# A planned order for the attention stage of a two-layer HGRN2 and dilated-attention block

## The chip, the core and the metric

The kernel runs on one core of a Trainium2 chip. Its time is the device time of one execution in microseconds. The engines named below are TensorE (PE, matrix products; its weight loads are PEld), VectorE (DVE), ScalarE (ACT), GpSimd (POOL) and SyncE (SP), whose queue issues most of the transfers from HBM.

## The reference, cut to what matters

One sequence of 512 tokens with 1024 channels goes through two layers. Each layer is a mixer and a gated feed-forward network (FFN), and each of the two is wrapped in a conditioned norm and a gate: six vectors per layer (shift, scale and gate for the mixer, the same for the FFN) come from the conditioning input and `ada_w`. They are written (layer, number) below, (1,4) for instance. Layer 0's mixer is HGRN2; layer 1's is attention in three groups:

```python
DILATED_GROUPS = ((128, 1), (512, 4), (2048, 16))      # window, dilation
def dilated_attention_mixer(u, cos, sin, w_in, w_out):
    proj = (u @ w_in).reshape(B, S, N_GROUPS, 3, ATT_HEADS, ATT_HEAD_DIM)
    for gi, (window, dilation) in enumerate(DILATED_GROUPS):
        q = apply_partial_rope(proj[:, :, gi, 0], cos, sin) * scale
        k = apply_partial_rope(proj[:, :, gi, 1], cos, sin)
        o_g, lse_g = dilated_group_attention(q, k, proj[:, :, gi, 2], window, dilation)
    wts = softmax(stack(lses), axis=0)                 # shares of the three groups
    o = einsum('gbsh,gbshd->bshd', wts, stack(outs))
    return o.reshape(B, S, D_MODEL) @ w_out

def swiglu_ffn(u, w_in, w_out):
    gate, up = split(u @ w_in, 2)
    return (silu(gate) * up) @ w_out
```

There are 8 heads of 128 channels. The rotary turn touches the first 32 of them. The FFN's inner width is 2816.

## The kernel before, in words

**Weights.** Each fp32 operand is split in a high half of type fp32r (a cast on ACT) and a low half (a subtraction on DVE), and each product is three products: high by high, high by low, low by high (`three`). The weights pass through a `Stream`: an item list in a fixed order, two raw buffers of 1 MB (`raw`), filled by SP, and three places of split weights (`hi`, `lo`). An item of kind `w` is a weight; `ada` is 1 MB of `ada_w`, which DVE reduces in four chunks into an accumulator (L257, L259); `do` and `rows` finish a conditioning vector. `weave(ws, others, first, every)` puts one of the others behind every so many weights. `take(ahead)` works through the items up to the weight wanted plus `ahead` more, by default two, and returns the split weight. So a plain `take()` also issues the splits of the next two weights.

**First FFN.** Its second product takes eleven weights, 48 products of 512 columns each. Between the first nine stand eight `ada` items, for (1,1) and (1,0).

**Attention stage.** Values of group 0 are made first. Values of groups 1 and 2 are made in two halves by a seven-product scheme (`seven_values`, L1395). Then, head by head and group by group, a block of 48 products makes query and key (24 each; `block` into a bank `mm`). `qk_evac` copies the rotary rows apart into `shared` (L1704) and the rest to `qk` (L1705), both on ACT. `turn_pair` turns the rows on DVE (L1712 to L1715), and ACT copies them back into `qk` (L1720 for group 0, L1722 for the other two). `scores` makes the scores (PE L1743, L1761 into a bank `a`), DVE takes the maxima (L1748, L1763), ACT the exponentials (L1753, L1772). `weights_of` computes the groups' shares (`wM`, `wE`, `wZ`, with an exponential on ACT, L1785), `merge_r` and `merge_n` scale by them on DVE (L1798, L1805), `flip` transposes on PE (L1810) and evacuates on ACT (L1815) or DVE (L1817), `pv_r` and `pv_n` sum over values (L1836, L1837, L1846, L1848) into `oT`. Each of these steps is put off by a fixed number of half blocks (`fl.add(n + 3, ...)`). The tile scheduler, which simulates a timeline while it emits (`schedule_with_timeline_sim`), sets the order of instructions on each engine here. The `ada` items of (1,2), (1,4) and (1,3) are woven in among the heads' weights.

**The seam.** `mixer_out` multiplies `oT` by `attn_w_out`, four weights. It makes the first five column blocks while head 7's last steps, given to it as `tail`, still run. Its order is fixed by hand. `cut(kt)` splits one column block of `oT` into `oh` (ACT, L434) and a low half (DVE, L435); `three` in this stage is L438 to L440:

```python
for kt in range(3):
    cut(kt)
for kt in range(KT):
    if kt % 4 == 0:
        w = st.take(0)
    ...
    for t in range(NT):
        prods(y0[t], t, kt, w)
```

and the loop over heads ahead of it takes its weights with `whi, wlo = st.take()`.

Of the kernel before, what the change touches and what calls it, by code (L numbers as in the profile page):

```python
# [1 line left out]

# [35 lines left out]
class Stream:  # L38
# [73 lines left out]
    def whole(self):  # L112

        assert self.items[self.done][0] in WHOLE
        self.fill()
        self.done += 1
        return self.raw.pop(self.done - 1)
# [10 lines left out]
    def take(self, ahead=None):  # L128
        ahead = self.parts - 1 if ahead is None else ahead
        k = min(self.taken + ahead, len(self.wpos) - 1)  # L130
        stop = next((i for i in range(self.done, len(self.items)) if self.items[i][0] in WHOLE), len(self.items))
        self.process_to(min(self.wpos[k] + 1, stop))
        if k == len(self.wpos) - 1:
            self.process_to(stop)
        self.taken += 1
        return self.ready.pop(0)

# [21 lines left out]
def block_kernel(tc, x, c, positions, ada_w, ada_b, norm_g, hgrn_w_in, lower, hgrn_norm_g, hgrn_w_out,  # L159
# [8 lines left out]
    with ExitStack() as ctx:  # L168
# [95 lines left out]
        def ada_item(l, v, hf, kq):  # L264
            src = ada_w[l, kq * 512:(kq + 1) * 512, v * D + hf * 512:v * D + (hf + 1) * 512]
            return ("ada", src.rearrange("(k p) n -> p k n", p=P), ada_chunk(l, v, hf, kq))
# [43 lines left out]
        def fin_item(l, v, hf):  # L310
            if v not in (2, 5):
                return ("do", None, col_fin(l, v, hf))
# [3 lines left out]
            return ("rows", (b, n), row_fin(l, v, hf))  # L316
# [62 lines left out]
        items += weave(f0b[:9], ada_seq((1, 1), (1, 0)), 0, 0.9) + f0b[9:]  # L379
# [4 lines left out]

        def aqk(g, hd):
            return ("w", tuple(AW[:, (g * 3 + k) * D + hd * P:(g * 3 + k) * D + (hd + 1) * P].rearrange(
                "(k p) n -> p k n", p=P) for k in range(2)))
# [14 lines left out]
        def woven(others, every):  # L402
            items.extend(weave(at, others, 0, every))
            at.clear()
# [6 lines left out]
        late = ada_seq((1, 2), (1, 4), (1, 3))  # L411
# [3 lines left out]
        woven(late[:8], 1.5)  # L415
# [4 lines left out]
        woven(late[8:], 1.3)  # L420
# [16 lines left out]
        def three(ps, ah, al, bh, bl, start, stop):  # L437
            pe.matmul(ps, ah, bh, start=start, stop=False)  # L438
            pe.matmul(ps, ah, bl, start=False, stop=False)  # L439
            pe.matmul(ps, al, bh, start=False, stop=stop)  # L440
# [942 lines left out]
        def seven_values(dsts, apart, th, tl):  # L1383


            C = lambda raw, c: V4(raw)[:, :, c * 256:c * 256 + 256]
            G = lambda t, o: V4(t[:, o * 1024:(o + 1) * 1024])
            u_of = lambda r, c: lambda kt, n: [a[:, r * 4 + kt, c * 256 + n * P:c * 256 + (n + 1) * P] for a in apart]
            t_of = lambda i: lambda kt, n: [a[:, i, kt, n * P:(n + 1) * P] for a in (th, tl)]
            raws, tiles = {}, {}  # L1390

            def cut(i, tile, o, k, c):
                hi, lo = tiles[i, tile]
                src = C(raws[i][k], c)
                act.copy(G(hi, o), src)  # L1395
                dve.tensor_sub(G(lo, o), src, G(hi, o).bitcast(F32))

            def place(i, tile):
                tiles[i, tile] = st.part_tiles(V0)

            def prepare(i, step):
                if i >= len(dsts):
                    return
                if step == 0:
                    raws[i] = [st.whole(), st.whole()]
                    place(i, 0)
                    cut(i, 0, 0, 0, 0)
                    cut(i, 0, 1, 1, 1)
                elif step == 1:
                    place(i, 1)  # L1410
                    cut(i, 1, 0, 1, 0)
                    a, b = raws[i]
                    dve.tensor_add(C(b, 1), C(b, 1), C(a, 1))
                    dve.tensor_add(C(a, 1), C(a, 1), C(a, 0))
                    dve.tensor_add(C(a, 0), C(a, 0), C(b, 1))
                    dve.tensor_add(C(b, 0), C(b, 0), C(a, 0))
                    cut(i, 1, 1, 0, 0)
                elif step == 2:
                    place(i, 2)
                    cut(i, 2, 1, 0, 1)  # L1420
                    st.fill(1)
                    cut(i, 2, 0, 1, 1)
                else:
                    place(i, 3)
                    cut(i, 3, 0, 1, 0)
                    raws.pop(i)
                    st.fill()

            def run(ps, i, tile, o, us):
                hi, lo = tiles[i, tile]  # L1430
                for n in range(2):
                    for kt in range(4):
                        w = slice(o * 1024 + kt * 256, o * 1024 + (kt + 1) * 256)
                        three(ps[:, n * 256:(n + 1) * 256], *us(kt, n), hi[:, w], lo[:, w], kt == 0, kt == 3)

            H2 = lambda a: a.rearrange("p (n c) -> p n c", n=2)
            for step in range(3):
                prepare(0, step)
            for i, dst in enumerate(dsts):
                X, Y, Z, U = (dst[:, t:t + 2, c:c + 256] for c in (0, 256) for t in (0, 2))  # L1440
                m1 = bank("mm")
                run(m1, i, 0, 0, u_of(0, 0))
                act.copy(X, H2(m1))
                m4 = bank("a")
                run(m4, i, 0, 1, t_of(2))
                prepare(i, 3)
                m2 = bank("mm")
                run(m2, i, 1, 0, u_of(1, 0))
                m6 = bank("mm")
                run(m6, i, 1, 1, t_of(3))  # L1450
                dve.tensor_add(Y, X, H2(m6))
                dve.tensor_add(X, X, H2(m2))
                prepare(i + 1, 0)
                m5 = bank("mm")
                run(m5, i, 2, 0, t_of(0))
                m7 = bank("mm")
                run(m7, i, 2, 1, t_of(1))
                dve.scalar_tensor_tensor(Z, Y, -1.0, H2(m7), op0=OP.mult, op1=OP.subtract)
                dve.tensor_add(Y, Y, H2(m5))
                dve.tensor_sub(U, Z, H2(m5))  # L1460
                dve.tensor_sub(Z, Z, H2(m4))
                prepare(i + 1, 1)
                m3 = bank("mm")
                run(m3, i, 3, 0, u_of(1, 1))
                dve.tensor_add(Y, Y, H2(m3))
                prepare(i + 1, 2)

# [383 lines left out]
        fl.n = 0  # L1851
        for kind, g, i in order:
            if kind == "v":
                if g == 1:

                    for fn in fl.at.pop(fl.n, []):
                        fn()
                    seven_values(V[1:], apart, th, tl)
                    if i:
                        act.dma_start(V[0], v_away)  # L1860
                continue
            if g == 0:
                heads[i] = {}
                n = fl.n
                fl.add(n + 3, lambda i=i: scores(i, 0))
                fl.add(n + 5, lambda i=i: scores(i, 1))
                fl.add(n + 7, lambda i=i: scores(i, 2))
                fl.add(n + 9, lambda i=i: (merge_r(i), merge_n(i)))
                fl.add(n + 10, lambda i=i: flips_r(i))
                fl.add(n + 11, lambda i=i: pv_r(i))  # L1870
                fl.add(n + 11, lambda i=i: flips_n(i))
                fl.add(n + 12, lambda i=i: pv_n(i))
# [8 lines left out]
        fl.at.clear()  # L1881
# [37 lines left out]
```

## Time and profile before

| | |
|---|---|
| runs | 1510.45, 1510.66 (median), 1511.49 us |
| profiled execution | 1511.44 us, of which the span takes 1509.4 |
| mean granted TensorE clock | 0.997 |
| first FFN's second product | about 537 to 649 us of the span |
| group 0's values | about 690 to 727 us |
| other values and heads | 727 to 1107 us |
| output product with head 7's end | from 1107 us |

Rows of a stretch read: from and to, length, then busy time (and instructions) of PE, PEld, DVE, ACT and POOL, the mean granted TensorE clock as a share of full speed, the share of time that the DMA engines were busy, GB/s. Timeline rows read: start, length, engine, line, operation and tiles, count, and in brackets the idle time ahead of it with what ended it. Rows of waits: what waited, for whom, us in total, times, the longest. Rows of groups: line, engine, operation, forms, count, busy us and mean ns, idle time before.

### The profile page before, as it was taken

To read this page: it belongs to the slowest core of one execution; us is meant where nothing else is said; L and a number is where in the kernel's file an instruction comes from. 1 tells how busy PE (TensorE), PEld (TensorE's weight loads), DVE (VectorE), ACT (ScalarE), POOL (GpSimd) and SP (SyncE) were. 2 spreads that over 40 slices of the span, in tenths; PEclk is the share of its full clock that TensorE was granted. 3 is DMA by queue.
4 is the path that set the end of the run, shared out by engine and by line. 5 is a ranking of instruction groups with operands and counts; after the bars stand their busy time and mean duration, and the time that the engine had idled before them with its cause. 6 is when DMAs were issued, how large, how long until landed. Compare 5 with 4: busy or idle time off the path is not lost. (4 is left out here: it accounts for less than half of the span.)

```text
span 1509.4 us, 23492 instructions
## 1 busy us (share of the span) xinstructions
PE 1493.7 (99%) x9231; PEld 1309.7 (87%) x9231; DVE 1040.2 (69%) x1807; ACT 746.6 (49%) x1321; POOL 199.0 (13%) x174
## 2 busy tenths in 40 slices
PE   8999999999999999999999999999999999999998
PEld 6777888898999988888988888988888899999886
DVE  4587768486888876577668766686466978887533
ACT  4443433362555542376546666356655555555231
POOL 1011211030111101040001110011002211110100
PEclk9999999999999999999999999999999999999999
DMA  9553444125333356424166540365213333334531
GB/s 309 166 183 126 156 152 168 56 85 167 101 109 107 107 200 213 155 108 141 57 183 191 151 120 29 123 185 141 84 52 117 100 97 112 112 112 141 199 108 56
DMA packets 206942, 199.14 MB, mean 132 GB/s; under 512 B 6840, under 2 KB 164720, under 8 KB 206576
## 3 DMA queue, kind: packets, MB, share of 16 engines
q1 hardware_dynamic: 203856, 190.87, 40.3%
q10 hardware_dynamic: 1952, 6.65, 1.2%
q8 instruction: 72, 1.18, 0.3%
q0 software_dynamic: 1024, 0.13, 0.2%
q14 instruction: 38, 0.31, 0.1%
HBM read 192.31 MB, written 5.31 MB: 131 GB/s over the span
## 5 line engine op out<-in xcount | busy, mean ns | idle before, releaser
L88 ACT CAST hi<-raw 128x2048 fp32r<-128x2048 f32 x68 | 129.7, 1907 | 199.1 <-DMA raw<-in_ffn_w_out_dram 60.8
L89 DVE TENSOR_TENSOR lo<-raw,hi 128x2048 fp32r<-128x2048 f32 x68 | 161.5, 2377 | 96.2 <-ACT hi L88 96.2
L438 PE MATMUL ps_mm<-apart,hi 128*128 128x512 f32 x384 | 151.4, 394 | 0.0
L439 PE MATMUL ps_mm<-apart,hi 128*128 128x512 f32 x384 | 151.2, 394 | 0.0
L440 PE MATMUL ps_mm<-apart,lo 128*128 128x512 f32 x384 | 150.6, 393 | 0.0
L438 PE MATMUL ps_mm<-uh,hi 128*128 128x512 f32 (+1 forms) x400 | 146.3, 366 | 0.0
L439 PE MATMUL ps_mm<-ul,hi 128*128 128x512 f32 (+1 forms) x400 | 144.3, 361 | 1.0 <-DVE ul L538 1.0
L440 PE MATMUL ps_mm<-uh,lo 128*128 128x512 f32 (+1 forms) x400 | 144.6, 361 | 0.0
L438 PE MATMUL ps_mm<-hi,oh 128*128 128x512 f32 x240 | 94.0, 392 | 0.0
L853 PE MATMUL ps_mm<-th,hiq 128*128 128x256 f32 x340 | 93.9, 276 | 0.0
L853 PE MATMUL ps_mm<-tl,hiq 128*128 128x256 f32 x340 | 93.9, 276 | 0.0
L853 PE MATMUL ps_mm<-th,loq 128*128 128x256 f32 x340 | 93.9, 276 | 0.0
L439 PE MATMUL ps_mm<-lo,oh 128*128 128x512 f32 x240 | 93.4, 389 | 0.0
L438 PEld LDWEIGHTS ps_mm<-uh,hi 128*128 128x128 f32 x400 | 75.5, 189 | 19.7 <-issue 8.4
L844 DVE TENSOR_TENSOR loq<-raw,hiq 128x1024 fp32r<-128x1024 f32 x68 | 80.2, 1221 | 16.8 <-ACT hiq L840 16.8
L439 PEld LDWEIGHTS ps_mm<-ul,hi 128*128 128x128 f32 x400 | 75.6, 189 | 12.1 <-DVE ul L538 1.4
L440 PEld LDWEIGHTS ps_mm<-uh,lo 128*128 128x128 f32 x400 | 75.5, 189 | 11.4
L824 POOL TENSOR_TENSOR raw<-raw 128x512 f32<-128x512 f32 x34 | 45.1, 1328 | 305.1 <-DVE spare L820 131.3
L440 PEld LDWEIGHTS ps_mm<-apart,lo 128*128 128x128 f32 x384 | 72.2, 188 | 14.5
L439 PEld LDWEIGHTS ps_mm<-apart,hi 128*128 128x128 f32 x384 | 72.2, 188 | 14.2
L438 PEld LDWEIGHTS ps_mm<-apart,hi 128*128 128x128 f32 x384 | 72.2, 188 | 14.1
L259 DVE SCALAR_TENSOR_TENSOR shared<-raw,cond,shared 128x512 f32<-128x512 f32 x98 | 73.2, 747 | 12.9 <-DMA raw<-in_ada_w_dram 11.9
(440 smaller groups left out, 4183.5 us busy)
## 6 DMA issues: line engine op xcount, KB each, us to landing
raw<-in_ada_w_dram SPq DMA_DIRECT2D x40, 1024.0 KB, 5.1
raw<-in_ffn_w_in_dram SPq DMA_DIRECT2D x136, 256.0 KB, 3.6
raw<-in_attn_w_in_dram SPq DMA_DIRECT2D x48, 512.0 KB, 5.1
raw<-in_ffn_w_out_dram SPq DMA_DIRECT2D x22, 1024.0 KB, 4.9
raw<-in_hgrn_w_in_dram SPq DMA_DIRECT2D x12, 1024.0 KB, 5.4
raw<-in_attn_w_in_dram SPq DMA_DIRECT2D x12, 1024.0 KB, 4.9
raw<-in_ffn_w_in_dram SPq DMA_DIRECT2D x10, 1024.0 KB, 5.0
first<-in_ada_w_dram SPq DMA_DIRECT2D x14, 512.0 KB, 7.9
```

Of the source, the lines that this page charges most:

```text
L88: self.nc.scalar.copy(hi, t)
L89: self.nc.vector.tensor_sub(lo, t, hi.bitcast(F32))
L259: dve.scalar_tensor_tensor(a, r[:, k], sc, a, op0=OP.mult, op1=OP.add)
L438: pe.matmul(ps, ah, bh, start=start, stop=False)
L439: pe.matmul(ps, ah, bl, start=False, stop=False)
L440: pe.matmul(ps, al, bh, start=False, stop=stop)
L824: pool.tensor_add(r[:, 2], r[:, 2], r[:, 0])
L844: dve.tensor_sub(lo, src, hi.bitcast(F32))
L853: pe.matmul(ps, w[x][:, a], us[kt][y], start=begin and kt + m == 0, stop=kt == 3 and m == 2, skip_group_check=True)
```

## The change

1. The attention stage behind group 0's values is no longer put out step by step. Each step is recorded in a `Plan` as a task with an engine, a cost, the tiles it reads and writes, and for TensorE a time by which it should start. `Plan.run` works out due times backwards and then places the tasks on PE, ACT, DVE, POOL, SP and DMA with one queue each, and the instructions are put out in that order, with the scheduler switched off for all engines including SP.
2. The turned rows of groups 1 and 2 go back into `qk` by DMA on SP's queue, 64 copies of 32 rows of 256 columns, instead of by ACT. Scaling by the shares goes from DVE to ACT, and so do the flip evacuations that DVE made. Weights in the stage are split in two halves of 1024 columns.
3. Vector (1,4), four `ada` loads of 1 MB and its finishing steps, moves from the heads into the second product of the first FFN.
4. After the plan the stream's position is set to `heads_end`. The plan itself ends with the last weight of head 7.

The numbers of products on TensorE and their kinds are those of before; `by_seven` is false for all groups, so that `sevens`, which would make query and key with fewer products, isn't used.

```diff
+class Plan:
+    LATE = {"PE": 0.55, "DMA": 0.3}
+    ...
+        for t in reversed(ts):
+            due = min([ts[o]["due"] - t["late"] for o in t["outs"]], default=1e9)
+            if t["goal"] is not None:
+                due = min(due, t["goal"] + t["cost"])
+            t["due"] = due - t["cost"]
+    ...
+                    able.sort(key=lambda i: (ts[i]["due"], i))
...
-        items += weave(f0b[:9], ada_seq((1, 1), (1, 0)), 0, 0.9) + f0b[9:]
+        items += weave(f0b, ada_seq((1, 1), (1, 0), (1, 4)), 0, 0.69)
...
+        by_seven = lambda g: False
...
-        late = ada_seq((1, 2), (1, 4), (1, 3))
+        late = ada_seq((1, 2), (1, 3))
...
-        woven(late[:8], 1.5)
+        woven(late[:6], 2)
...
-        woven(late[8:], 1.3)
+        woven(late[6:], 2)
+        heads_end = len(items)
         items += [wtok(attn_w_out[0], kq, hf * 512) for hf in range(2) for kq in range(2)]
...
-            whi, wlo = st.take()
-            pair = []
-            for k in range(2):
-                ps = block(whi, wlo, k * D, P, u=apart)
-                heads[i]["qk"[k], g] = qk_evac(ps, g, k, pair)
-                if k == 1:
-                    turn_pair(g, pair)
-                fl.tick()
...
+        def COPY(fn, r=(), w=()):
+            plan.add("SP", 0.1, lambda e: fn(), r, w, late=2.4)
...
+            if g:
+                for i, t in enumerate((q, k)):
+                    for n in range(2):
+                        o = (2 * i + n) * 32
+                        COPY(lambda t=t, n=n, o=o: nc.sync.dma_start(t.t[0:32, n * 256:n * 256 + 256], rows.t[o:o + 32]),
+                             [rows(2 * i + n)], [t(n)])
+                return
...
+            e = shares(st_["sR"], st_["oR"], rr_)
+            for r in range(NT):
+                ACT(0.42, lambda r=r: act.activation(st_["PR"][:, r], st_["PR"][:, r], AF.Copy, scale=e.t[:, 0, r:r + 1]),
+                    [e(0)], [("PR", 0, 1, r), ("PR", 0, 2, r)])
...
+        while at_item[0] < heads_end:
+            condition(st.items[at_item[0]])
+            at_item[0] += 1
+        with tc.manual_schedule(engines=ORDERED | {mybir.EngineType.SP}):
+            planned = plan.run()
+        st.done, st.taken = heads_end, st.taken + sum(k == "qk" and not by_seven(g) for k, g, _ in order)
```

SP's queue in the first FFN's second product, from the load that is issued at 567.25 us of before's span, before the change:

```order
L68 DMA raw_5185<-in_ffn_w_out_dram 128x2x1024
L68 DMA raw_5290<-in_ada_w_dram 128x4x512
L68 DMA raw_5296<-in_ffn_w_out_dram 128x2x1024
L68 DMA raw_5358<-in_ada_w_dram 128x4x512
L68 DMA raw_5364<-in_ffn_w_out_dram 128x2x1024
L68 DMA raw_5437<-in_ada_w_dram 128x4x512
L68 DMA raw_5443<-in_ffn_w_out_dram 128x2x1024
L68 DMA raw_5505<-in_ada_w_dram 128x4x512
L68 DMA raw_5511<-in_ffn_w_out_dram 128x2x1024
```

and after it, from the same place on the queue; the last row is the same weight, the ninth of the eleven, as the last row above:

```order
L69 DMA raw_5185<-in_ada_w_dram 128x4x512
L69 DMA raw_5290<-in_ffn_w_out_dram 128x2x1024
L69 DMA raw_5296<-in_ada_w_dram 128x4x512
L69 DMA raw_5302<-in_ffn_w_out_dram 128x2x1024
L69 DMA raw_5375<-in_ada_w_dram 128x4x512
L69 DMA raw_5381<-in_ada_w_dram 128x4x512
L69 DMA raw_5443<-in_ffn_w_out_dram 128x2x1024
L69 DMA raw_5459<-in_ada_w_dram 128x4x512
L69 DMA raw_5465<-in_ffn_w_out_dram 128x2x1024
L69 DMA raw_5527<-in_ada_w_dram 128x4x512
L69 DMA raw_5533<-in_ada_w_dram 128x4x512
L69 DMA raw_5605<-in_ffn_w_out_dram 128x2x1024
```

The ninth weight is eight loads behind the first row before, and eleven after.

ACT at the seam, before: from the cast of the second output weight (`hi_9952`; the first, `hi_9829`, stands a few rows further ahead) to the `oh` casts of the first three column blocks, with some rows of head 7 left out between the two fences. First the place of the casts among head 7's rows:

```order
L88 CAST hi_9829<-raw_9604 128x2048
L1704 ACTIVATE shared<-ps_mm_9771 32x256 x2
L1705 ACTIVATE qk_9796<-ps_mm_9771 128x512
L1772 ACTIVATE h,sR_9707<-h,nR_9708 128x256 x4
L1785 ACTIVATE wE_9903<-wE_9903 128x8
L1720 COPY qk_9758<-shared 32x2x128 x2
L1720 COPY qk_9796<-shared 32x2x128 x2
L1704 ACTIVATE shared<-ps_mm_9835 32x256 x2
L1705 ACTIVATE qk_9860<-ps_mm_9835 128x512
L88 CAST hi_9952<-raw_9731 128x2048
```

and then the seam itself:

```order
L434 CAST oh_10074<-oT_6047 128x512
L434 CAST oh_10075<-oT_6048 128x512
L434 CAST oh_10076<-oT_6049 128x512
L1838 COPY oT_late_6053<-ps_b_10037 128x4x128
L1815 COPY h<-ps_a_10052 128x512
L1722 COPY qk_9983<-shared 32x256 x2
L1722 COPY qk_10024<-shared 32x256 x2
L1772 ACTIVATE h,sR_10059<-h,nR_10060 128x256 x4
L434 CAST oh_10138<-oT_6050 128x512
```

After the change the same place on ACT reads:

```order
L570 CAST oh_10113<-oT_6095 128x512
L89 CAST hi_10130<-raw_9715 128x2048
L2375 COPY oT_late_6099<-ps_b_9811 128x4x128
L2359 COPY h<-ps_a_10053 128x384
L2359 COPY h<-ps_a_10061 128x512
L1823 ACTIVATE h,sR_9630<-h,nR_9599 128x256 x4
L570 CAST oh_10181<-oT_6096 128x512
...
L1836 ACTIVATE wE_10220<-wE_10220 128x8
L1680 DMA h<-h_away 128x1024
L570 CAST oh_10184<-oT_late_6099 128x512
L1836 ACTIVATE wE_10252<-wE_10252 128x8
L89 CAST hi_10267<-raw_9813 128x2048
```

Both casts of output weights have moved from inside head 7 to behind its steps: the first behind the `oh` casts, the second behind both exponentials of the shares. DVE's rows show the low halves at the matching places, the first behind three `oT` steps, the second behind the last scaling by the shares:

```order
L571 TENSOR_TENSOR oT_10127<-oT_6095,oh_10113 128x512
L90 TENSOR_TENSOR lo_10131<-raw_9715,hi_10130 128x2048
L2297 ISA h,mR_9567<-ps_a_10097,maskR 128x128
...
L1856 TENSOR_SCALAR h<-h,wE_10252 128x128
L1856 TENSOR_SCALAR h<-h,wE_10252 128x256 x3
L90 TENSOR_TENSOR lo_10268<-raw_9813,hi_10267 128x2048
```

On TensorE the first product of the stage reads `hi_10130`, and, four score products later, the second reads `lo_10131`; the fifth column block reads `hi_10267` and `lo_10268`.

SP's queue among the heads before, where it held loads alone:

```order
L66 DMA raw_7030<-in_attn_w_in_dram 128x8x128 x2
L68 DMA raw_7117<-in_ada_w_dram 128x4x512
L66 DMA raw_7123<-in_attn_w_in_dram 128x8x128 x2
L66 DMA raw_7217<-in_attn_w_in_dram 128x8x128 x2
L62 DMA raw_7224<-in_ada_b_dram 128x512
```

and after, with the copies of turned rows between them:

```order
L69 DMA raw_7144<-in_ada_w_dram 128x4x512
L67 DMA raw_7183<-in_attn_w_in_dram 128x8x128 x2
L2027 DMA qk_6485<-shared 32x256 x2
L2027 DMA qk_6486<-shared 32x256 x2
L67 DMA raw_7235<-in_attn_w_in_dram 128x8x128 x2
L69 DMA raw_7259<-in_ada_w_dram 128x4x512
```

Copies now stand between loads on the one queue.

More of the change, by code (lines that the diff above doesn't have):

```diff
@@ L1381, in tok_proj @@
                 done(t, ps)
[L1383 to L1466, printed above, removed]
@@ new lines, in POOL, with load_next, make @@
+        def POOL(cost, fn, r=(), w=(), **k):
+            plan.add("POOL", cost, lambda e: fn(), r, w, **k)
+        def COPY(fn, r=(), w=()):
+            plan.add("SP", 0.1, lambda e: fn(), r, w, late=2.4)
+        def load_next():
+            def make():
+                while st.items[st.loaded][1] is None:
+                    st.raw[st.loaded] = None
+                    st.loaded += 1
+                st._load(st.loaded)
+                st.loaded += 1
+                return st.raw[st.loaded - 1]
+            p = plan.place("raw", 2, make)
+            plan.add("DMA", 3.4, None, w=[p()], late=2.2)
+            queue.append(p)
@@ new lines, in next_weights, with split_place, products, go @@
+        def next_weights():
+            while True:
+                item = st.items[at_item[0]]
+                at_item[0] += 1
+                if item[0] in ("w", "quarters", "half"):
+                    return queue.pop(0)
+                condition(item)
+        def split_place(first):
+            return plan.place("hl", 3, lambda: st.part_tiles(first))
+        def products(cost, dst, key, terms, begin, reads):
+            def go():
+                todo = [p for t in terms() for p in t]
+                for i, (x, y) in enumerate(todo):
+                    pe.matmul(dst(), x, y, start=begin and i == 0, stop=i == len(todo) - 1, skip_group_check=True)
+            PE(cost, go, reads, [key])
@@ new lines, in flipped, with go, make @@
+        def flipped(hd, name, which, ts, hf):
+            st_ = heads[hd]
+            src = st_[which]
+            b = mm_of("a")
+            reads = [("PR", 0, hf + 1, t) for t in ts] if which == "PR" else [("PN", hd % 2, t) for t in ts]
+            def go():
+                for t in ts:
+                    pe.transpose(b.t[:, t * P:(t + 1) * P], src[:, t, hf * P:(hf + 1) * P], ident)
+            PE(0.114 * len(ts), go, reads, [b()])
+            def make():
+                flip_no[0] += 1
+                return h[:, 3, flip_no[0] % 2 * 512:flip_no[0] % 2 * 512 + 512]
+            pt = plan.place("pt", 2, make)
+            o = ts[0] * P
+            ACT(0.6, lambda: act.copy(pt.t[:, o:], b.t[:, o:]), [b()], [pt()])
+            st_[name] = pt
@@ L1852, in block_kernel @@
+        steps = []
         for kind, g, i in order:
             if kind == "v":
[L1854 to L1872, printed above, removed]
@@ new lines, in block_kernel @@
+        ahead = 0
+        for n, (kind, g, hd, k, prepare, go) in enumerate(steps):
+            while ahead < min(len(steps), n + 3):
+                steps[ahead][4]()
+                ahead += 1
+            if kind == "qk" and g == 0:
+                begin_head(hd)
+            if kind == "v" and (n == 0 or steps[n - 1][0] != "v"):
+                for fn in ticks.at.pop(ticks.n, []):
+                    fn()
+            go()
+            if kind == "qk" and by_seven(g):
+                ticks.tick()
```

520 lines of the change are left out of this document (508 added, 12 removed).

## The prediction

> **What bounds the kernel now.** I read the page first, then busy time by stretches, then TensorE's waits, then the timelines of the two places where the change reorders weights. Of the page, the span and the engines:
>
> ```profile
> span 1509.4 us, 23492 instructions
> PE 1493.7 (99%) x9231; PEld 1309.7 (87%) x9231; DVE 1040.2 (69%) x1807; ACT 746.6 (49%) x1321; POOL 199.0 (13%) x174
> L88 ACT CAST hi<-raw 128x2048 fp32r<-128x2048 f32 x68 | 129.7, 1907 | 199.1 <-DMA raw<-in_ffn_w_out_dram 60.8
> L259 DVE SCALAR_TENSOR_TENSOR shared<-raw,cond,shared 128x512 f32<-128x512 f32 x98 | 73.2, 747 | 12.9 <-DMA raw<-in_ada_w_dram 11.9
> raw<-in_ada_w_dram SPq DMA_DIRECT2D x40, 1024.0 KB, 5.1
> ```
>
> TensorE is busy 99% of the span. By stretch (first FFN's second product, the heads, the seam into the output product):
>
> ```profile
> 537.00:649.00 112.00, 112.00 (x499) 92.75 (x498) 76.32 (x132) 37.53 (x48) 15.04 (x7) 1.00 0.53 181
> 727.00:1107.00 380.00, 378.84 (x2195) 332.82 (x2195) 251.73 (x677) 217.97 (x432) 40.30 (x36) 1.00 0.43 128
> 1107.00:1136.00 29.00, 29.00 (x170) 25.22 (x169) 19.37 (x60) 14.68 (x30) 1.32 (x2) 1.00 0.24 76
> ```
>
> In all three TensorE has no room: 1.16 us idle in the 380 us of heads, none in the others, while DVE has 128 us free there and ACT 162. TensorE's waits in the heads, all of them:
>
> ```profile
> PE ps_a L1743 <- ACT qk L1720: 0.6, 1, 0.6
> PE ps_b L1837 <- ACT h L1815: 0.3, 1, 0.3
> PE ps_b L1846 <- ACT h L1815: 0.2, 1, 0.2
> ```
>
> So a better order can win at most the 1.16 us, because the order rows list 8647 TensorE instructions in both kernels, of the same kinds. The path of sevens (`by_seven`) is switched off. Every weight that comes late costs TensorE in full, and nothing after it gives the time back.
>
> **The heads.** Removed: the 1.1 us of waits; the plan puts each evacuation ahead of the product that reads it, so I take −1.1. Off the path: ACT loses 64 row copies and gains the scaling and half the flip evacuations; DVE loses those. With 162 and 128 us free, a change of some tens of us on either engine costs nothing by itself. The copies now go through SP's queue. Their chain, from the seam's rows:
>
> ```profile
> 1105.13 0.76 ACT L1704 ACTIVATE shared<-ps_mm 32x256 f32<-32x256 f32 x2 [1.67 <-PE ps_mm L440]
> 1105.92 0.44 DVE L1712 STREAM_SHUFFLE rot<-shared 128x256 f32<-128x256 f32 x1
> 1108.26 0.41 DVE L1715 TENSOR_TENSOR shared<-shared,rot 128x256 f32<-128x256 f32 x1
> scr<-sN POOLq DMA_DIRECT2D x8, 4.0 KB, 3.7
> ```
>
> Row evacuation 0.8, four DVE steps of about 0.42 (1.7), then a landing. The trace has no 32 KB copy inside SBUF; the nearest rows are a 4 KB transfer (3.7 us) and a 1 MB one (5.1 us, above), so 3.7 to 5.1, and I take 5.1 since it queues with such loads: 7.6 us from the block's end. The score that reads it stands two projection blocks later, 48 products of 0.227 us (spacing below), 10.9 us. Cover 3.3 us, cost 0; if two loads stand ahead of it on SP, 5.1 us more, the score waits 1.8 us. Behind a copy that waits on SP for DVE's rows stand the next loads, held by at most those 2.5 us; the split waits for them, and TensorE for the split. Three places hold split weights, so two weights, 10.9 us of products each, lie ahead: 0.
>
> **The conditioning vector in the first FFN.** SP's queue there, and DVE's last split of the ninth weight:
>
> ```profile
> 567.25 0.37 SPq L68 DMA_DIRECT2D raw<-in_ffn_w_out_dram  x1
> 571.36 0.37 SPq L68 DMA_DIRECT2D raw<-in_ada_w_dram  x1
> 600.52 0.37 SPq L68 DMA_DIRECT2D raw<-in_ada_w_dram  x1
> 605.33 9.80 SPq L68 DMA_DIRECT2D raw<-in_ffn_w_out_dram  x3
> 612.44 2.29 DVE L89 TENSOR_TENSOR lo<-raw,hi 128x2048 fp32r<-128x2048 f32 x1 [2.91 <-ACT hi L88]
> 537.31 0.40 PE L438 MATMUL ps_mm<-hi,oh 128*128 128x512 f32 x1
> ```
>
> Between 567.25 and 605.33 stand 8 issues: 4.76 us each, with two buffers. The ninth weight, issued at 605.33, is split at 614.7: 9.4 us. TensorE starts at 537.3 and takes 48 products, 10.9 us, per weight, so it wants the ninth at 537.3 + 8 × 10.9 = 624.5: 9.8 us of slack. In the new order (the SP rows shown with the change) the load at 567.25 is a conditioning one, and the ninth weight is the 11th issue behind it. At 4.76 each: 567.25 + 52.4 + 9.4 = 629.0, 4.5 us late. But a conditioning load holds a buffer for less: 5.1 + 4 × 0.75 = 8.1 us against 9.4, and 7 of the 11 are such: (7 × 8.1 + 4 × 9.4) / 2 = 47.2, ready at 623.8, just in time. Ends 0 and 4.5; I take +3.0, nearer the slow one, since the 8 measured issues (half of each kind, 4.4 by that rule) ran at 4.76. Taking the vector out of the heads frees DVE there, which is worth nothing.
>
> **The seam.** This is the large term. In before, the loop over heads calls `st.take()`, which splits two weights ahead, so the first two weights of the output product were split inside the last head. In after, the plan stops at `heads_end`, and `mixer_out`'s `st.take(0)` issues these splits where it needs them: the first behind the three `oh` casts, the second behind both exponentials of head 7's shares. The rows that price it:
>
> ```profile
> 1091.53 1.91 ACT L88 CAST hi<-raw 128x2048 fp32r<-128x2048 f32 x1 [1.14 <-PE ps_mm L439]
> 1106.53 1.66 ACT L434 CAST oh<-oT 128x512 fp32r<-128x512 f32 x3
> 1123.77 0.21 ACT L1785 ACTIVATE wE<-wE 128x8 f32<-128x8 f32 x1 [2.24 <-DVE wE L1784]
> 1093.89 2.29 DVE L89 TENSOR_TENSOR lo<-raw,hi 128x2048 fp32r<-128x2048 f32 x1
> 1108.59 1.48 DVE L435 TENSOR_TENSOR oT<-oT,oh 128x512 fp32r<-128x512 f32 x2
> 1124.89 1.08 DVE L1805 TENSOR_SCALAR h<-h,wE 128x128 f32<-128x128 f32 x4
> 1107.39 0.47 PE L438 MATMUL ps_mm<-hi,oh 128*128 128x512 f32 x1
> 1112.79 1.06 PE L1761 MATMUL ps_a<-qk,qk 128*128 128x128 f32 x8
> 1113.60 0.48 PE L438 MATMUL ps_mm<-hi,oh 128*128 128x512 f32 x1
> 1121.85 0.39 PE L438 MATMUL ps_mm<-hi,oh 128*128 128x512 f32 x1
> 1124.35 0.39 PE L440 MATMUL ps_mm<-hi,oT 128*128 128x512 f32 x1
> ```
>
> From 1121.85 to 1124.35 stand 11 steps, 0.227 us each. The split's prices are 1.91 (ACT) and 2.29 (DVE).
>
> First split: the `oh` casts end at 1108.19; the cast behind them ends at 1110.10, and TensorE's first product, at 1107.39 before, waits 2.7 us. One product (0.23) and four score products (0.8, from 1112.79 to 1113.60) later it wants the low half at 1111.1. DVE is free of the `oT` steps at 1110.07, so the low half ends at 1112.4: 1.3 us more. Together 4.0; what follows moves with TensorE.
>
> Second split: TensorE comes to the fifth column block at 1121.85. The last exponential ends at 1123.98, the cast behind it at 1125.9: 4.05 us. The low half begins when head 7's last scaling ends, 1125.97, and ends at 1128.26; TensorE, one product on, waits from 1126.1: 2.1 us. Together 6.2. Seam: +10.2; I give it 7 (engines arriving earlier than before's times) to 14 (each of the four waits about 1 us longer, since evacuations stand between the casts).
>
> These gaps may also cost clock. From the start of the kernel:
>
> ```profile
> 14.54 0.63 PE L1146 MATMUL ps_mm<-ident,late 128*128 128x128 f32 x4 [1.69 <-DVE cols L1176]
> 12.00:16.00 4.00, 2.18 (x18) 1.82 (x17) 2.41 (x8) 3.78 (x8) 1.69 (x3) 0.93 1.13 328
> 16.00:20.00 4.00, 3.68 (x13) 2.79 (x14) 3.82 (x7) 2.24 (x5) 0.66 (x1) 0.50 1.13 328
> 20.00:30.00 10.00, 9.37 (x61) 6.18 (x59) 4.83 (x9) 2.75 (x4) 0.73 (x1) 0.89 1.12 333
> ```
>
> The second to last number is DMA's share, the one before it the granted clock: after a gap of 1.69 us among sparse work it fell to 0.50 and came back within the next ten. Lost there: 4 × 0.07 + 4 × 0.50 + 10 × 0.11 = 3.4 us. What falls while TensorE waits is free, and a slow stretch after the first split only eats into the second wait. So 0 to 3.4 for the second gap; I take 2.2. [...]
>
> **Sum**, against the profiled execution's 1511.44 us: −1.1 (heads) + 3.0 (first FFN) + 10.2 (seam) + 2.2 (clock) = +14.3: 1525.7. That execution lies 0.8 above the median of the runs, so 1525 for the median.
>
> **Rivals.** *The seam is covered.* If the engines ran the casts early, because ACT and DVE, freer in the last head, reach them before TensorE ends its last block, only −1.1 is left and the first FFN's low end, 0: 1510.3, no change. For it: DVE and ACT are two thirds busy at most. Against: both stand in fixed order behind work that waits for TensorE's own results. It decides only if the first cast ends 2.7 us and the second low half 6.4 us earlier. A share of the 256-column products at a tighter spacing might bring it below −3, but no row shows a reason. 0.09 together.
>
> *The copies come late.* If two loads stand ahead of a copy in most heads, 16 blocks wait up to 1.8 us: +29, and half of that, +14, if every second does: 1540. Speaking for it: SP's new rows put loads directly ahead of copies. Against: 3.3 us of cover for one load, and DMA's share is 0.43. [...] 0.12.
>
> *The stream in the first FFN becomes the bound*: its full 4.5 us, and the next weights late by as much again since the same buffers feed them: +9.0 in place of 3.0, 1531. The slack of 9.8 us is all there is. 0.12.
>
> **How the numbers follow.** Forecast 0.67, late copies 0.12, stream 0.12, not slower 0.09. The low end is the seam at 7 with −1.1 and nothing else, 1516.5 for the median, rounded to 1515 to let in a little more; the high end is 14 + 3.4 + 4.5 − 1.1 = +20.8, 1531.5, stretched to 1534 for the stream's case. Outside lie most of the late copies and the covered seam, 0.2. A measurement of this kernel tells about 0.2%, 3.0 us, from no change. Faster by more 0.04, within 0.06, slower 0.90.
>
> **What would show it.** Right: in the changed profile TensorE waits at the first products of the output product on the `hi` cast and the low half, about 4 us, and at the fifth column block about 6 us, with a granted clock below 1.00 in the stretch behind. The heads' 380 us are 378 to 380. The first FFN's stretch is about 3 us longer, with waits on the low half of the sixth to eleventh weight. Wrong: no wait on those casts at the seam, or waits of score products on SP's copies, or a stretch of the first FFN that is as long as before.

## The result and the profile after

The changed kernel takes 1526.8 us (median; 1525.01 to 1528.42) against 1510.6, a ratio of 1.0097 with the 95% interval 1.0085 to 1.0109. The forecast was 1525, range 1515 to 1534. The profiled execution has a span of 1526.3 us, 16.9 more than before. The page of the changed kernel, in the rows that answer to those of before:

```profile
span 1526.3 us, 23645 instructions
PE 1499.9 (98%) x9231; PEld 1314.9 (86%) x9231; DVE 1031.1 (68%) x1760; ACT 751.3 (49%) x1350; POOL 199.1 (13%) x174
```

TensorE has the same 9231 instructions and is busy 6 us longer on them, so some ran slower, and it stood idle about 11 us more. Busy time by stretch, changed kernel, the stretches of the prediction:

```profile
537.00:649.00 112.00, 110.24 (x487) 90.70 (x487) 88.13 (x162) 36.15 (x44) 20.38 (x7) 1.00 0.64 216
727.00:1107.00 380.00, 378.63 (x2192) 333.73 (x2191) 223.62 (x589) 219.21 (x459) 34.31 (x33) 1.00 0.40 117
1107.00:1136.00 29.00, 22.21 (x109) 18.29 (x107) 16.06 (x57) 12.94 (x25) 1.87 (x3) 0.85 0.19 59
```

The seam has lost 6.8 of 29 us to idleness and runs at a granted clock of 0.85; the first FFN lost 1.8; the heads are where they were. TensorE's waits from 537 to 1142 us, changed kernel:

```profile
PE ps_mm L574 <- ACT hi L89: 6.0, 2, 3.8
PE ps_mm L575 <- DVE lo L90: 3.4, 3, 1.6
PE ps_a L2294 <- ACT h L2359: 2.1, 2, 1.4
PE ps_mm L655 <- DVE xn L649: 1.3, 2, 0.8
```

To put a size on each stretch I take the same TensorE instructions in both timelines. Before (the start of the FFN's product, 537.31, and of the output product, 1107.39, stand in the prediction): the first transposes of the norm behind the FFN, the first value product, and the norm behind the output product:

```profile
648.86 0.60 PE L519 MATMUL ps_mm<-ident,xn 128*128 128x128 f32 x4
671.61 0.47 PE L438 MATMUL ps_mm<-hi,uh 128*128 128x512 f32 x1
1151.44 0.82 PE L519 MATMUL ps_b<-ident,xn 128*128 128x128 f32 x6
```

The same five instructions of the changed kernel; the fourth begins after a wait of 2.26, so TensorE came to it at 1110.99:

```profile
537.38 0.40 PE L574 MATMUL ps_mm<-hi,oh 128*128 128x512 f32 x1
651.29 0.60 PE L655 MATMUL ps_mm<-ident,xn 128*128 128x128 f32 x4
675.58 0.48 PE L574 MATMUL ps_mm<-hi,uh 128*128 128x512 f32 x1
1113.25 0.57 PE L574 MATMUL ps_mm<-hi,oh 128*128 128x512 f32 x1 [2.26 <-ACT hi L89]
1168.70 1.03 PE L655 MATMUL ps_b<-ident,xn 128*128 128x128 f32 x8
```

| stretch | before | changed | difference | forecast |
|---|---|---|---|---|
| first FFN, second product | 111.55 | 113.91 | +2.4 | +3.0 |
| norm behind it | 22.75 | 24.29 | +1.5 | 0 |
| values and heads | 435.78 | 435.41 | −0.4 | −1.1 |
| seam, output product | 44.05 | 57.71 | +13.7 | +12.4 (10.2 waits, 2.2 clock) |

The sum is +17.2; the part behind is 0.3 shorter, which makes it the span's 16.9. The largest term is the forecast one, in its place; one term of 1.5 us was not seen. That the total lies within 2 us of 1525 is in part luck: at the seam the waits came to 8.4 us where 10.2 were forecast and the low clock to 5.0 where 2.2 were, and these two misses offset each other.

### The profile page after: what moved, and what is told of

Read it like the earlier page. It is cut to its first block, busy times and chain, and to the rows that moved or that the text cites. A ratio compares the mean times of both kernels' runs of the same rounds, so it can differ in the third digit from the quotient of the medians.

```text
span 1526.3 us, 23645 instructions
## 1 busy us (share of the span) xinstructions
PE 1499.9 (98%) x9231; PEld 1314.9 (86%) x9231; DVE 1031.1 (68%) x1760; ACT 751.3 (49%) x1350; POOL 199.1 (13%) x174
## 3 DMA queue, kind: packets, MB, share of 16 engines
q0 software_dynamic: 1024, 0.13, 0.2%
## 5 line engine op out<-in xcount | busy, mean ns | idle before, releaser
L2007 PE MATMUL ps_mm<-apart,hiq 128*128 128x512 f32 x736 | 231.2, 395 | 0.0
L2007 PEld LDWEIGHTS ps_mm<-apart,hiq 128*128 128x128 f32 x736 | 135.8, 188 | 26.5
L89 ACT CAST hi<-raw 128x2048 fp32r<-128x2048 f32 x45 | 85.8, 1907 | 142.4 <-DMA raw<-in_ffn_w_out_dram 70.0
L90 DVE TENSOR_TENSOR lo<-raw,hi 128x2048 fp32r<-128x2048 f32 x45 | 107.6, 2392 | 53.5 <-ACT hi L89 53.4
L2007 PE MATMUL ps_mm<-apart,loq 128*128 128x512 f32 x368 | 143.7, 390 | 0.0
L576 PEld LDWEIGHTS ps_mm<-uh,lo 128*128 128x128 f32 x400 | 75.5, 189 | 11.5
L2007 PEld LDWEIGHTS ps_mm<-apart,loq 128*128 128x128 f32 x368 | 69.1, 188 | 14.8
L976 ACT CAST hiq<-raw 128x1024 fp32r<-128x1024 f32 x68 | 68.0, 1047 | 17.5 <-DVE raw L964 16.7
L2159 ACT ACTIVATE shared<-ps_mm 32x256 f32<-32x256 f32 x96 | 35.6, 371 | 71.4 <-PE ps_mm L2007 70.3
L576 PE MATMUL ps_mm<-hi,ol 128*128 128x512 f32 x176 | 68.5, 389 | 0.0
```

Of the source, the lines that this page charges most:

```text
L89: self.nc.scalar.copy(hi, t)
L90: self.nc.vector.tensor_sub(lo, t, hi.bitcast(F32))
L576: pe.matmul(ps, al, bh, start=False, stop=stop, skip_group_check=part)
L976: act.copy(hi, src)
L2007: pe.matmul(dst(), x, y, start=begin and i == 0, stop=i == len(todo) - 1, skip_group_check=True)
L2159: ACT(0.38, lambda hf=hf, o=o: act.activation(rows.t[o:o + 32], b.t[0:32, hf * 256:hf * 256 + 256], AF.Copy, scale=scale), [b()], [rows(2 ...
```

## The experiments

Each ratio below is to runs of before made beside that experiment. Their medians were 1514.0 us (splits put back, late splits, vector, both undone), 1512.8 (transposes, copies on ACT, fewer products) and 1513.4 (order alone), against 1510.6 above, so totals from different groups don't subtract to a few us. The kernel's start alone moves by 3 us: the first FFN's second product begins between 535.2 and 538.5 us in the eleven traces, though no edit touches what stands ahead of it. Differences of a few us are therefore taken from the same TensorE instructions in two traces, as in the table.

**The splits put back.** The first two output weights become tasks of the plan, with a time by which they should start; everything else is the changed kernel.

```diff
+        for _ in range(2):
+            raw = next_weights()
+            p = plan.place("hl", 3, lambda: st.part_tiles(0))
+            goal = clock[0] - 12.0
+            plan.add("ACT", 2.0, ..., goal=goal)      # hi
+            plan.add("DVE", 2.3, ..., goal=goal)      # lo
+            done_with_raw()
...
-        st.done, st.taken = heads_end, ...
+        st.done, st.taken = heads_end + 2, ...
```

> After, with the first two output weights split inside the plan, in head 7, as before had them; nothing else differs. Theory (the seam, by where the splits stand): the five waits on these halves vanish, with the low clock behind them, 13.9 us by the two traces' offsets: 1526.8 - 13.9 = 1513 us, no wait on hi or lo at the output product, clock 1.00 in the stretch 1107 to 1136. Rival (the plan's own order in the heads, with DMA copies, makes the engines late at the seam): the waits move to other operands there and less than half comes back, 1520 or more.

It took 1514.6 us, ratio to before 1.0011 (1.0002 to 1.0021). The stretch from 1107 to 1142 us in its profile:

```profile
1107.00:1142.00 35.00, 35.00 (x205) 30.60 (x205) 20.57 (x63) 17.16 (x37) 2.63 (x4) 1.00 0.29 92
```

No idle time, clock 1.00: the seam's cost is gone, and the plan's other rows there don't bring it back. The rival falls. By the table's marks the seam and output product take 43.96 us, 13.75 less than in the changed kernel. Of the five waits counted in the expectation, two stand in the first FFN and stay. The span is 13.6 shorter than the changed kernel's: the first FFN lost 3.6 more (below), and an earlier start and the norm gave 3.2 back. That the median lies 1.6 above 1513 is within the spread of its runs (1512.59 to 1518.47).

**Before, with late splits.** The other direction, on the old scheduler and without any plan:

```diff
-            whi, wlo = st.take()
+            whi, wlo = st.take(max(0, 2 - g) if i == NH - 1 else None)
```

> Before, with head 7's last two weights taken with 1 and 0 ahead in place of 2, so that the two output weights are split where the output product takes them; nothing else differs. Theory (the seam): the same cost as in the changed kernel, 10 us of waits and 3 to 4 us of low clock: 1510.6 + 13.9 = 1524.5 us. Rival (the plan's order makes the seam's wait, not the late split alone): before's engines reach the casts earlier and the cost is under 7 us, below 1518.

It took 1526.0 us, ratio 1.0092 (1.0071 to 1.0113), the theory's number. TensorE's waits from 537 to 1142 us in it:

```profile
PE ps_mm L438 <- ACT hi L88: 3.8, 1, 3.8
PE ps_mm L439 <- DVE lo L89: 3.4, 2, 1.8
PE ps_a L1761 <- DVE h L1817: 1.3, 2, 1.0
```

and the stretch 1107 to 1142 with its clock:

```profile
1107.00:1142.00 35.00, 26.70 (x125) 21.50 (x124) 18.99 (x60) 15.26 (x30) 1.88 (x3) 0.85 0.24 76
```

One argument in one line costs about as much as the whole change: from the first value product to the norm behind the output product this trace takes 494.3 us where before takes 479.8, 14.4 more. The first wait of size is here on the low half (1.8) and not on the cast, so the cost comes in other parts but to the same sum. With the run before, the seam's cost is shown to be where two splits stand, and not the plan's order.

**The clock at the seam.** The splits stay late, and TensorE is given transposes to work through while it waits:

```diff
                         if kt % 4 == 0:
                             w = st.take(0)
+                            spare = y0[0] if kt == 0 else bank("b")
+                            for _ in range(20 if kt == 0 else 36):
+                                pe.transpose(spare[:, 0:P], ident, ident)
```

> After, with 20 transposes of the identity put ahead of the output product's first product and 36 ahead of its fifth column block (into a bank that is overwritten or spare), 0.11 us each, so that TensorE works through most of the two long waits; the splits stand as late as in the changed kernel. Theory (idle TensorE loses its clock at the seam, 3.4 us of the 13.9): the granted clock stays 1.00 there, the waits stay, 1526.8 - 3.4 = 1523.4 us. Rival (the low clock isn't brought by these gaps, or the transposes don't hold it): no change, 1526 to 1528.

First the changed kernel's seam in short stretches (the second to last but one number is the granted clock):

```profile
1110.00:1113.00 3.00, 0.99 (x10) 0.75 (x8) 2.73 (x6) 3.00 (x4) 0.00 (x0) 1.00 0.05 11
1116.00:1120.00 4.00, 4.00 (x13) 3.23 (x12) 0.93 (x8) 0.00 (x0) 0.00 (x0) 0.50 0.75 262
1131.00:1135.00 4.00, 0.60 (x3) 0.17 (x1) 3.50 (x17) 1.76 (x3) 0.00 (x0) 0.88 0.42 132
1135.00:1138.00 3.00, 1.01 (x2) 0.51 (x3) 2.73 (x4) 0.33 (x1) 0.00 (x0) 0.50 0.00 0
1138.00:1142.00 4.00, 4.00 (x13) 3.17 (x14) 0.00 (x0) 0.00 (x0) 0.00 (x0) 0.64 0.71 247
```

and the same places with the transposes:

```profile
1116.00:1120.00 4.00, 3.10 (x16) 2.46 (x17) 3.22 (x9) 1.84 (x4) 0.00 (x0) 1.00 0.25 37
1135.00:1138.00 3.00, 1.17 (x9) 0.78 (x7) 2.99 (x5) 0.61 (x1) 0.00 (x0) 1.00 0.00 0
1138.00:1142.00 4.00, 3.95 (x21) 3.38 (x22) 0.69 (x1) 0.20 (x1) 0.00 (x0) 1.00 0.69 222
```

In the changed kernel a full stretch of 4 us holds 13 products after each gap, as against 17 or 18 at the usual 0.227 us; with the transposes the clock stays at 1.00 in all of them. From the first value product to the norm behind the output product the trace takes 3.9 us less than the changed kernel's. The total shows little of it: 1525.2 us, ratio 1.0082 (1.0061 to 1.0102), an interval that holds the changed kernel's 1.0097, and in its trace the first FFN and the norm, untouched, lost 1.6 more and the start came 1.1 later. So the low clock here is brought by the gaps, and useless work in them holds it at 1.00. The theory stands on the clock's rows and the matched stretch, not on the total.

**The vector (1,4).** Before, with the list of the changed kernel:

```diff
-        items += weave(f0b[:9], ada_seq((1, 1), (1, 0)), 0, 0.9) + f0b[9:]
+        items += weave(f0b, ada_seq((1, 1), (1, 0), (1, 4)), 0, 0.69)
...
-        late = ada_seq((1, 2), (1, 4), (1, 3))
+        late = ada_seq((1, 2), (1, 3))
...
```

> Before, with only the conditioning vector (1,4) moved into the first FFN's second product and out of the heads. Theory (two raw buffers, eleven loads ahead of the ninth weight where eight were): +2.4 us of waits on the low halves there and +1.5 us of waits of the norm's transposes on DVE behind it, 1514.5 us. Rival (those waits come from other parts of the change): within 1 us of before, 1510 to 1511.5.

It took 1515.1 us, ratio 1.0011 (1.0000 to 1.0021). TensorE's waits in it, the same kinds that the changed kernel has in this place:

```profile
PE ps_mm L439 <- DVE lo L89: 2.9, 2, 1.8
PE ps_mm L519 <- DVE xn L513: 1.5, 2, 0.8
```

The mechanism is shown: waits of the kind and place foreseen come with the list alone. By the table's marks the FFN's product takes 115.48 us and the norm 24.43, 3.9 and 1.7 more than before, where 2.4 and 1.5 were expected; the heads, freed of the four loads, gain 0.3. The total doesn't show it: the runs of before beside it spread from 1510.5 to 1515.8 us with a median of 1514.0, so that the ratio barely tells this edit from none. In the run with the splits put back the same code waited

```profile
PE ps_mm L575 <- DVE lo L90: 3.1, 2, 1.8
628.00:636.00 8.00, 8.00 (x30) 6.41 (x29) 5.33 (x7) 2.38 (x2) 3.60 (x1) 0.79 0.71 259
```

and after the longer wait (1.8 us) the mean clock of 8 us fell to 0.79 (30 products, where the changed kernel has 37 in such a stretch), some 1.6 us more. But the vector's run has a wait of 1.8 us at the same place, and behind it

```profile
628.00:636.00 8.00, 8.00 (x37) 6.60 (x36) 5.16 (x7) 2.44 (x2) 3.60 (x1) 1.00 0.74 257
```

the clock held; so the length of the wait alone doesn't decide (see the clock, below). In the changed kernel's own profile the two waits are 1.28 and 0.48 and the clock held too. In the traces of the four kernels with this list, the FFN's product and the norm together lost 3.9 us (changed kernel), 5.6 (vector alone), 5.5 (transposes) and 6.2 (splits put back, with the low clock).

**Both undone.** Splits back in head 7 and the vector back among the heads; the planned order and the DMA copies stay.

> After, with the output weights split in head 7 and the vector (1,4) back among the heads (both undone). Theory: 1526.8 - 13.9 - 3.9 = 1509.0 us, that is 1.6 below before by a planned order of the heads alone. Rival (the heads' plan has less room when the vector's loads are back in it): the heads lose what the FFN gains, 1512 to 1514.

It took 1507.0 us, ratio 0.9960 (0.9948 to 0.9972): faster than both kernels. Its heads:

```profile
727.00:1107.00 380.00, 380.00 (x2210) 335.31 (x2209) 241.49 (x628) 224.88 (x464) 40.30 (x36) 1.00 0.46 134
```

TensorE doesn't wait once between 537 and 1142 us. From the first value product (670.04) to the output product (1103.41)

```profile
670.04 0.47 PE L574 MATMUL ps_mm<-hi,uh 128*128 128x512 f32 x1
1103.41 0.47 PE L574 MATMUL ps_mm<-hiq,oh 128*128 128x512 f32 x1
```

are 433.4 us, 2.4 less than before. That is what the planned order, with the work it moves between engines, is worth; the changed kernel got 0.4 of it, and 1.37 of the rest is one score that waited there for ACT to empty a flip's bank. Expected were 1509.0, and the other 2 us of its trace come from places that the change doesn't touch: its first FFN's product starts 1.6 us earlier than before's, as in several of these runs, and the part behind the output product is 0.3 shorter.

**What in the plan does it.** Row copies back on ACT, on top of both undone (`COPY(` becomes `ACT(0.41, ` with `act.copy`):

> The kernel with both undone (output weights split in head 7, vector (1,4) among the heads), and the 64 copies of turned rows done by ACT at 0.4 us each as in before, in the planned order. Theory (copies by DMA are covered and ACT has room, so where the copies run is worth nothing): same as that kernel within 1 us, no TensorE wait in the heads. Rival (the DMA copies are what removes the heads' waits): 1 to 3 us slower, waits of scores on ACT's copies.

1507.9 us, ratio 0.9969 (0.9958 to 0.9981), no wait in the heads, 433.7 us from the first value product to the output product against 433.4: the same. Where the copies run is worth nothing here. Then also the scaling by the shares and the flips' first halves back on DVE, so that only the order is left of the change:

> The kernel with both undone, and with all work of the heads back on the engines of before: row copies on ACT, scaling by the shares and the flips' first halves on DVE. What is left of the change is the planned order (and the weights' splits in two halves). Theory (the order, not the change of engines, removes the heads' waits): as with both undone, 1507 to 1508 us, no TensorE wait in the heads. Rival (ACT and DVE had to be rebalanced for the plan to work): waits on DVE's scaling or flip copies come back, 1509 us or more.

1509.7 us, ratio 0.9980 (0.9969 to 0.9990). One wait came back in the heads,

```profile
PE ps_a L2294 <- DVE h L2362: 1.0, 1, 1.0
```

a score behind DVE's copy of a flip, and the stretch from the first value product to the output product takes 435.1 us, 1.7 more than with both undone and 0.7 less than before. My theory was wrong here, the rival right: the order alone is not free of waits. The run moves the scaling and the flips back together; the wait stands behind a flip, and which of the two costs the other 0.7 us stays open.

**Fewer products.** The heads are bound by TensorE, so the code for seven products instead of eight was switched on, for group 2 and then for groups 1 and 2 (`by_seven = lambda g: g == 2`, `g > 0`), on top of both undone:

> The kernel with both undone, and query and key of group 2 by seven products of 256 columns (84 for each pair instead of 48 of 512). Theory (TensorE bounds the heads and the other engines have room): 8 x (48 x 0.227 - 84 x 0.120) = 6.5 us less, up to 8 x (10.9 - 84 x 0.1137) = 10.8 if the 256-column products run at their tightest spacing. Rival (ACT and DVE, with the additional splits and sums, or the row copies, become the bound): TensorE waits on splits or on the sums, and the gain is under 3 us.

> As the one before, for groups 1 and 2. Theory: twice that, 13 to 22 us less than with both undone. Rival: DVE, at 63% in the heads, is passed, and the gain per group falls to under half of that of group 2 alone.

1514.6 us and 1518.2 us, ratios 1.0016 (1.0004 to 1.0027) and 1.0038 (1.0026 to 1.0050): slower by 7.6 and 11.2 than without, and by 7.7 and 10.8 in the traces from the first value product to the norm behind the output product. TensorE's waits in the heads of the first:

```profile
PE ps_mm L2007 <- ACT ps_mm L2092: 6.2, 5, 3.3
PE ps_mm L2007 <- ACT ps_mm L2096: 1.8, 2, 1.4
PE ps_a L2351 <- DVE sN L2274: 1.4, 1, 1.4
```

Both theories fell, and the waits are of the rival's kind. In a chain of seven products some add to a bank that ACT has just filled with a copy of another (L2092, L2096), so TensorE waits on ACT's place in its queue though ACT is busy 62% of that time. Against the forecast the first lost 14.2 us in its trace: 11.5 are idle time, where both undone had none, and the mean granted clock of its profiled execution, 0.997 against 0.998, stands for some 1.5 us more (an estimate, 0.001 of the span of 1512.5). What is left, about 1, is the saving itself, some 5.5 in place of 6.5.

## Why the prediction was right, and where not

**The bound.** Nothing after a late weight gives the time back: from the norm behind the output product on, both kernels keep nearly the same distance, 17.26 us at 1151.44 against 1168.70, and the span is 16.9 longer. Shown.

**First split.** Forecast 2.7 us of wait for the high half and 1.3 for the low one. Measured 2.26, then 0.74 for a score, and nothing of size for the low half. The second wait's cause was misread: behind the late cast on ACT stood the evacuation of a flip, and the score, one product on, needed that bank. I had named the order of ACT's rows and not asked who waits for the evacuations behind the cast.

**Second split.** Forecast 4.05 and 2.1. Measured, in the changed kernel:

```profile
1135.38 0.80 PE L574 MATMUL ps_mm<-hi,oh 128*128 128x512 f32 x1 [3.78 <-ACT hi L89]
1137.78 0.80 PE L575 MATMUL ps_mm<-lo,oh 128*128 128x512 f32 x1 [1.60 <-DVE lo L90]
```

Right in cause and size. The steps that end them, the last exponential and the last scaling by the shares, are the ones named:

```profile
1133.34 0.21 ACT L1836 ACTIVATE wE<-wE 128x8 f32<-128x8 f32 x1 [2.24 <-DVE wE L1835]
1133.45 1.88 ACT L89 CAST hi<-raw 128x2048 fp32r<-128x2048 f32 x1
1134.46 1.07 DVE L1856 TENSOR_SCALAR h<-h,wE 128x128 f32<-128x128 f32 x4
1135.45 2.28 DVE L90 TENSOR_TENSOR lo<-raw,hi 128x2048 fp32r<-128x2048 f32 x1
```

**The clock.** Forecast 2.2, all behind the second gap, chosen between 0 and the 3.4 us lost at the kernel's start; the 2.2 itself stands in no row. The four waits are 8.4 us of the stretch's 13.7; the rest, some 5, is low clock. The changed kernel's clock stood at half for two stretches:

```profile
1113.54:1120.36 6.82, 6.08 (x19) 4.93 (x19) 2.92 (x9) 1.45 (x3) 0.00 (x0) 0.50 0.48 164
1134.02:1140.84 6.82, 3.85 (x8) 2.79 (x9) 3.62 (x7) 1.31 (x1) 0.00 (x0) 0.50 0.23 76
```

Half of TensorE's busy time in them is lost: 3.0 us behind the first gap and 1.9 behind the second. The second is near the 2.2 taken. The step that failed is "a slow stretch after the first split only eats into the second wait". The eleven products and the score behind the first gap ran slow too, which put off the next score (1122.35), and the last exponential hangs on that one: the second wait's chain moved with them. The clock fell 0.3 us after the gap of 2.26 us, ahead of the one of 0.74. The gap of 1.69 us at the kernel's start had brought half clock too, and the run with transposes shows that here it is the gap.

What parts the gaps with half clock behind them from those without can be read from the clock's records in the traces of before and of the changed kernel, though no run was made to test it. All changes of the clock in each of the two lie multiples of 3.41 us apart. Cut both into windows at that step: of 876 that ran at full clock, the six with TensorE busy for 1.74 us or less (1.16 ahead of the drop at 1113.54, 1.00 ahead of that at 1134.02; two stand at the kernels' ends) were all followed by half clock, and of those with 2.05 or more none was. The wait of 1.28 us in the first FFN lay in a window with 2.13 busy, 601.54 to 604.95, and the clock held. That such windows also part the two waits of 1.8 us in the first FFN, with 0.79 behind the one and 1.00 behind the other, was not shown.

**First FFN.** Eleven issues take 567.08 to 616.95 us, 4.53 us each:

```profile
567.08 0.37 SPq L69 DMA_DIRECT2D raw<-in_ada_w_dram  x1
616.95 0.37 SPq L69 DMA_DIRECT2D raw<-in_ffn_w_out_dram  x1
624.55 2.29 DVE L90 TENSOR_TENSOR lo<-raw,hi 128x2048 fp32r<-128x2048 f32 x1 [0.57 <-ACT hi L89]
```

between the 4.3 and 4.76 of the two ends; the ninth weight is ready at 626.8, forecast 623.8 to 629.0. The term of +3.0 measured +2.4 in that profile, most of it earlier than forecast: 1.28 of wait at the seventh weight (604.35) and 0.48 at the ninth. What the sum lacked is the norm behind it, +1.5. On DVE the split of the first value weight stands ahead of the layer's update (`yg`) in both kernels, before:

```profile
637.40 2.29 DVE L89 TENSOR_TENSOR lo<-raw,hi 128x2048 fp32r<-128x2048 f32 x1 [6.26 <-ACT hi L88]
640.94 0.69 DVE L483 TENSOR_TENSOR yg<-ps_mm,gate 128x512 f32<-128x512 f32 x1 [1.24 <-ACT junk L474]
```

and in the changed kernel:

```profile
642.94 2.29 DVE L90 TENSOR_TENSOR lo<-raw,hi 128x2048 fp32r<-128x2048 f32 x1 [2.54 <-ACT hi L89]
645.15 0.68 DVE L619 TENSOR_TENSOR yg<-ps_mm,gate 128x512 f32<-128x512 f32 x1
```

The split comes 5.5 us later with its load, the update behind it 4.2 us later, of which 2.4 is TensorE's own delay, and two transposes wait on what follows from it, 0.53 and 0.78 us. The order was there to be read in DVE's rows; I followed the weights and not what DVE does between them.

**Heads.** The forecast −1.1 was the whole of the waits that the profile of before shows; the change got −0.4, since a new wait took the place:

```profile
907.72 0.49 PE L2294 MATMUL ps_a<-qk,qk 128*128 128x128 f32 x2 [1.37 <-ACT h L2359]
```

With both undone 2.4 was to be had, so "a better order can win at most the 1.16 us" was wrong too. The other 1.2 us is not idle time, of which before's stretch has 1.16 us in all: so TensorE's products there stand slightly closer together, by the two lengths (433.4 against 435.8), and no row shows it singly. Why they do stays open.

**The copies.** The rival of late copies didn't come. The trace prices them in the heads at

```profile
qk<-shared SPq DMA_DIRECT2D x60, 32.0 KB, 1.9
```

against the 3.7 to 5.1 taken. A 32 KB copy inside SBUF lands sooner than the 4 KB transfer taken as the low end (1.9 us against 3.7). By the byte it is dear: a 1 MB load, 32 times the bytes, lands in 5.1 us, under three times as long. But with 10.9 us of products ahead of the score, a landing that is covered costs nothing.

## What to carry to other kernels

When a loop is replaced, look at what its last calls did for the stage behind it: an iterator that works two items ahead hides its split in the old loop, and stopping it at the border exposed both splits on the bound engine. A wait's price on TensorE was not its length here: the gap of 2.26 us had 6.83 us at half clock behind it, that of 1.28 us none. So price the clock as a possibility, and follow who hangs on the slowed products. Freeing an engine that is a third idle and not the bound (DVE in the heads) bought nothing, and moving its work to a place with less than one weight's slack (9.8 us) did cost.

## What the runs showed of the hardware

Behind a gap of 2.26 us TensorE's granted clock stood at 0.50 for 6.83 us (1113.54 to 1120.36 in the changed kernel). Behind a wait of 1.8 us the mean clock of 8 us was 0.79 in the run with the splits put back and 1.00 in the vector's run, and behind one of 1.28 us it was 1.00 in the changed kernel. In the traces of before and of the changed kernel each of the four stretches of half clock ahead of the kernel's end lasted 6.83 us, and it followed 3.41 us in which TensorE was busy for at most 1.74. Transposes of the identity, whose result nobody reads, held the clock at 1.00 at the seam. A copy of 32 rows of 1 KB inside SBUF on SP's queue landed in 1.9 us (median of the 60 in the heads; 6.1 at most of all 64), with loads of 0.5 and 1 MB on the same queue.
